# FFN down projection: three instead of two pairs per half as block products, their operands in two tiles each, and the turn of the PSUM sets advanced at each half's end

## The chip, the core and the metric

The kernel runs on one core of a Trainium2 chip. The metric is the time of one execution on the device, in microseconds (us); lower is better. TensorE (PE) multiplies matrices, VectorE (DVE) and ScalarE (ACT) work element by element, GpSimd (POOL) has little to do here, and SyncE (SP) issues the DMAs in the order in which they stand in its queue. Each engine takes its instructions in program order and waits on semaphores.

## The reference

Two decoder layers over 256 tokens of width 2048, in fp32. Layer 0 mixes tokens by sparse attention, layer 1 by an mLSTM; each is followed by a feed-forward part (FFN) of width 8192, and that part is what the change touches:

```python
hn = rms_norm(h, norm_ffn[i])
h = h + jnp.square(jax.nn.relu(hn @ ffn_w_up[i])) @ ffn_w_down[i]
```

## The kernel before

The program is written with a tile framework: tiles come from pools with a fixed number of buffers, a new tile of a tag waits until the oldest one of that tag is read for the last time, and a scheduler sets the order of the instructions on each engine at build time. So matmuls of different pairs may stand interleaved on PE, as long as their operands' order allows it.

Every fp32 product is made of three fp32r products: `split` makes a high part on ACT (a cast, L136) and a low part on DVE (a subtraction, L137), and PE multiplies high by high, high by low and low by high, each as a matmul of 128x512.

The FFN of a layer goes in four **quarters** of 2048 of its 8192 hidden columns. For each quarter, four calls of `project_t` make the up projection of 512 hidden columns each; their results leave PSUM as eight **pairs** of 256 hidden columns (`lhs`). Then the down projection of the quarter runs in two **halves** of 1024 output columns (`down_chunk`): a first half and a second half. In a half the eight pairs are added up in four PSUM banks `C` (2 token blocks x 2 column blocks of 512).

- A **plain pair** takes two loads of 512 KB (`w`, 5 buffers), each split into `wh` and `wl` (4 buffers each), and 24 matmuls (L494 to L496).
- A **block pair** (its number stands in `SEVEN`) takes one load of 1 MB (`sw`, one buffer) and a two-by-two block scheme with 7 products instead of 8: three subtractions on DVE make the sums of weight blocks (`st`, L478 to L480), `split` makes `sh` and `sl` of the 4 blocks in `sw` and of the 3 in `st`, and 21 matmuls follow. Three of its products go to `C` and four to a second set of banks, `S`, which all block pairs of a half share. After the half's last block pair, `S` is combined into a tile `e` and added to the residual `h` (`early`, L526 to L530 and L578). Tile `e` has the tag of `sw`, so it stands in the one buffer of `sw`.

The eight PSUM banks are two sets of four, `acc` and `acx`. `banks()` hands them out in turn by flipping `turn[0]`; a `project_t` takes one set, a half takes two (`C`, then `S`). At the end of a half, `C` is added to `h` (L274, in the last quarter L568 to the output).

The last quarter of layer 0's FFN goes without block pairs (`mix` is false), in four calls of `project`. So 7 quarters have halves, 14 in all. The loads for the first block pair of a quarter are issued during the up projection before it.

Of the kernel before, what the change touches and what calls it, by code (L numbers as in the profile page):

```python
# [10 lines left out]
F32R = mybir.dt.float32r  # L11
# [5 lines left out]
P = 128  # L17
# [14 lines left out]
TAKEN = -3.4e38  # L32
OUT = -1.0e30
RC, IC = 32, 16
SEVEN = (2, 5)


@with_exitstack
def trunk_kernel(ctx: ExitStack, tc, x, norm_mix, norm_ffn, att_w_in, att_q_gain, att_k_gain,
# [14 lines left out]
    n = [0]  # L54

    def uid(s):
        n[0] += 1
        return f"{s}_{n[0]}"
# [76 lines left out]
    def split(hi, lo, src):  # L135
        nc.scalar.copy(hi, src)  # L136
        nc.vector.tensor_tensor(lo, src, hi.bitcast(F32), op=ALU.subtract)  # L137
# [35 lines left out]
    turn = [0]  # L173
# [283 lines left out]
    def ffn(nm, up, down, nxt, pool, last=False):  # L457
# [14 lines left out]
        def seven(down, r0, n0):  # L472

            w = pool.tile([P, 4, 512], F32, tag="sw", name=uid("sw"))
            nc.sync.dma_start(w.rearrange("p (k n) f -> p k (n f)", k=2),
                              down[r0:r0 + 256, n0:n0 + 1024].rearrange("(k p) f -> p k f", p=P))
            t = pool.tile([P, 3, 512], F32, tag="st", name=uid("st"))
            nc.vector.tensor_tensor(t[:, 0:2], w[:, 1::2], w[:, 0:2], op=ALU.subtract)  # L478
            nc.vector.tensor_tensor(w[:, 1], w[:, 3], t[:, 0], op=ALU.subtract)
            nc.vector.tensor_tensor(t[:, 2], w[:, 2], w[:, 1], op=ALU.subtract)  # L480
            hi = pool.tile([P, 7, 512], F32R, tag="sh", name=uid("sh"))
            lo = pool.tile([P, 7, 512], F32R, tag="sl", name=uid("sl"))
            split(hi[:, :4], lo[:, :4], w)
            split(hi[:, 4:], lo[:, 4:], t)
            return hi, lo

        def down_chunk(lhs, q, n0, early, evac):

            C = banks()
            S = None  # L490
            first, final = min(SEVEN), max(SEVEN)

            def three(o, ah, al, hi, lo, start, stop):
                nc.tensor.matmul(o, ah, hi, start=start, stop=False, skip_group_check=True)  # L494
                nc.tensor.matmul(o, ah, lo, start=False, stop=False, skip_group_check=True)  # L495
                nc.tensor.matmul(o, al, hi, start=False, stop=stop, skip_group_check=True)  # L496

            for p in range(8):
                r0 = q * 2048 + 256 * p
                if p not in SEVEN:  # L500
                    a = lhs[p]
                    for k in range(2):
                        w = wp.tile([P, 2, 512], F32, tag="w", name=uid("w"), bufs=5)
                        nc.sync.dma_start(w, down[r0 + P * k:r0 + P * (k + 1), n0:n0 + 1024].rearrange(
                            "p (n f) -> p n f", n=2))
                        wh = wp.tile([P, 2, 512], F32R, tag="wh", name=uid("wh"), bufs=4)
                        wl = wp.tile([P, 2, 512], F32R, tag="wl", name=uid("wl"), bufs=4)
                        split(wh, wl, w)
                        for m in range(2):
                            ms = slice(m * P, (m + 1) * P)  # L510
                            for n in range(2):
                                three(C[2 * m + n], a[:, 0, k, ms], a[:, 1, k, ms], wh[:, n], wl[:, n],
                                      p == 0 and k == 0, p == 7 and k == 1)
                    continue
                if p == first:
                    S = banks()
                hi, lo = seven(down, r0, n0)
                vh, vl = lhs[p]

                for o, s, b, own in ((C[2], 2, 2, 0), (S[0], 0, 0, 1), (C[3], 6, 3, 0), (S[2], 4, 1, 1),  # L520
                                     (S[1], 3, 4, 1), (S[3], 5, 5, 1), (C[0], 1, 6, 0)):
                    three(o, vh[:, s], vl[:, s], hi[:, b], lo[:, b], bool(own and p == first), bool(own and p == final))
                if p == final:
                    e = pool.tile([P, 4, 512], F32, tag="sw", name=uid("e"))
                    u2 = t2k([P, 512], F32, "u2")
                    nc.scalar.copy(e[:, 2], S[0])  # L526
                    nc.vector.tensor_tensor(u2, S[2], e[:, 2], op=ALU.add)
                    nc.vector.tensor_tensor(e[:, 3], S[1], u2, op=ALU.add)
                    nc.vector.tensor_tensor(e[:, 0], S[3], u2, op=ALU.add)
                    nc.vector.tensor_tensor(e[:, 1], S[1], e[:, 0], op=ALU.add)  # L530
                    for m in range(2):
                        early(m, e[:, 2 * m:2 * m + 2])
            for m in range(2):
                for n in range(2):
                    evac(m, n, C[2 * m + n])

        for q in range(4):
            lhs, half = [], []
# [2 lines left out]
            def evac_up(b, p):  # L541
# [5 lines left out]
                if b % 2 == 0:  # L547
                    return
                if mix and len(lhs) in SEVEN:
                    y4 = pool.tile([P, 8, P], F32, tag="y4", name=uid("y4"))  # L550
# [207 lines left out]
    n0 = Norm(0)  # L758
# [53 lines left out]
```

## Time and profile before

| what | value |
|---|---|
| time, median of 3 runs | 2133.13 us (2132.56 to 2135.68) |
| the profiled execution's own time | 2133.99 us |
| its span in the profile | 2131.7 us |
| busy PE / DVE / ACT | 2114.1 us (99%) / 1424.9 us (67%) / 1045.3 us (49%) |
| mean granted clock of PE | 0.998 |

The span runs from the first to the last instruction; some 2.3 us lie around it. Matmuls are pipelined: a record of a 128x512 matmul lasts about 390 ns, while one follows the other after about 230 ns. So the busy time of PE hides what one matmul costs; it is read from a stretch with a known number of matmuls.

### The profile page before, as it was taken

The page shows a single profiled execution, that of the slowest core. Times are in us where ns is not written, and L with a number is a line of the kernel's source. Part 1 is how long each engine was busy: PE and PEld are TensorE (multiplying, and loading weights), DVE is VectorE, ACT ScalarE, POOL GpSimd, SP SyncE. Part 2 cuts the span into 40 slices and gives each one's busy share as a digit, 9 for nine tenths or more (in the row PEclk, how much of TensorE's full clock was granted, in tenths as well). Part 3 has the DMA queues.
Part 4 walks back from the last instruction along what each step waited for, and adds up shares of the span by engine and source line. Part 5 has one row for each costly group of instructions (what it writes and reads, how often), then busy time and mean ns, then how long its engine had stood idle before and what let it go on. Part 6 is the DMA issues. An engine that isn't in the chain of part 4 may idle for free.

```text
span 2131.7 us, 27757 instructions
## 1 busy us (share of the span) xinstructions
PE 2114.1 (99%) x10664; PEld 1797.7 (84%) x10664; DVE 1424.9 (67%) x1962; ACT 1045.3 (49%) x1350; POOL 14.0 (1%) x20
## 2 busy tenths in 40 slices
PE   9999999999999999999999999999999999999999
PEld 8988888888888888888999888888878888878887
DVE  5697676668668667655654565766677577668666
ACT  6556554544444454444554545545445444444543
POOL 0000000000000000000011000000000000000000
PEclk9999999999999999999999999999999999999999
DMA  7665366656655755665567655566567556656654
GB/s 233 188 180 151 118 213 188 191 171 213 190 168 186 219 173 176 188 188 186 169 183 210 171 167 169 192 201 190 160 196 215 179 183 207 188 162 217 190 164 142
DMA packets 178803, 393.06 MB, mean 184 GB/s; under 512 B 12336, under 2 KB 29168, under 8 KB 178672
## 3 DMA queue, kind: packets, MB, share of 16 engines
q1 hardware_dynamic: 178624, 391.29, 59.4%
q8 instruction: 83, 1.36, 0.3%
q14 instruction: 48, 0.39, 0.1%
q10 hardware_dynamic: 48, 0.02, 0.0%
HBM read 389.16 MB, written 2.10 MB: 184 GB/s over the span
## 4 chain that ended last, share of the span: by engine, by line
PE 94%; DMA 3%; DVE 2%; issue 1%; ACT 0%; SPq 0%; DVEq 0%
PE acc L195 13%; PE acx L195 12%; PE acc L168 10%; PE acc L167 10%; PE acc L169 10%; PE acc L494 7%; PE acc L495 7%; PE acc L496 7%; PE acx L197 6%; PE acc L197 6%; DMA sw<-in_ffn_w_down_dram 2%; PE acx L496 1%; PE acx L495 1%; PE acx L494 1%; DVE h L578 1%
## 5 line engine op out<-in xcount | busy, mean ns | idle before, releaser
L137 DVE TENSOR_TENSOR wl<-w,wh 128x1024 fp32r<-128x1024 f32 (+3 forms) x696 | 834.4, 1204 | 558.6 <-ACT wh L136 554.4
L136 ACT CAST wh<-w 128x1024 fp32r<-128x1024 f32 (+3 forms) x696 | 715.9, 1033 | 857.2 <-PE acc L496 229.3
L195 PE MATMUL acc<-xT,wh 128*128 128x512 f32 x1152 | 399.1, 396 | 4.4 <-DVE h L274 4.4
L195 PE MATMUL acx<-xT,wh 128*128 128x512 f32 x1152 | 402.3, 394 | 0.0
L197 PE MATMUL acx<-xT,wl 128*128 128x256 f32 x1152 | 321.0, 280 | 0.0
L197 PE MATMUL acc<-xT,wl 128*128 128x256 f32 x1152 | 312.4, 280 | 0.0
L495 PE MATMUL acc<-wl,hT 128*128 128x512 f32 x672 | 262.7, 391 | 0.0
L494 PE MATMUL acc<-wh,hT 128*128 128x512 f32 x672 | 259.9, 392 | 2.6 <-DVE h L274 2.2
L496 PE MATMUL acc<-wh,hT 128*128 128x512 f32 x672 | 262.1, 390 | 0.0
L195 PEld LDWEIGHTS acc<-xT,wh 128*128 128x128 f32 x1152 | 214.2, 188 | 55.0 <-issue 6.4
L195 PEld LDWEIGHTS acx<-xT,wh 128*128 128x128 f32 x1152 | 215.7, 187 | 49.6
L197 PEld LDWEIGHTS acx<-xT,wl 128*128 128x128 f32 x1152 | 217.1, 189 | 0.3
L197 PEld LDWEIGHTS acc<-xT,wl 128*128 128x128 f32 x1152 | 214.6, 189 | 3.0
L167 PE MATMUL acc<-wh,xT 128*128 128x512 f32 (+3 forms) x576 | 212.6, 372 | 2.1 <-ACT xT L230 2.1
L168 PE MATMUL acc<-wl,xT 128*128 128x512 f32 (+3 forms) x576 | 212.6, 371 | 0.0
L169 PE MATMUL acc<-wh,xT 128*128 128x512 f32 (+3 forms) x576 | 211.9, 371 | 0.0
L494 PEld LDWEIGHTS acc<-wh,hT 128*128 128x128 f32 x672 | 126.1, 188 | 34.4 <-issue 5.3
L495 PEld LDWEIGHTS acc<-wl,hT 128*128 128x128 f32 x672 | 126.2, 188 | 27.6 <-DVE wl L137 1.5
L496 PEld LDWEIGHTS acc<-wh,hT 128*128 128x128 f32 x672 | 126.2, 188 | 26.7
L167 PEld LDWEIGHTS acc<-wh,xT 128*128 128x128 f32 x576 | 108.1, 188 | 15.1 <-ACT xT L230 2.5
L169 PEld LDWEIGHTS acc<-wh,xT 128*128 128x128 f32 x576 | 108.3, 188 | 12.9 <-issue 0.3
L168 PEld LDWEIGHTS acc<-wl,xT 128*128 128x128 f32 x576 | 108.3, 188 | 12.8 <-issue 0.7
(242 smaller groups left out, 2237.6 us busy)
## 6 DMA issues: line engine op xcount, KB each, us to landing
w<-in_ffn_w_up_dram SPq DMA_DIRECT2D x256, 512.0 KB, 3.8
w<-in_ffn_w_down_dram SPq DMA_DIRECT2D x200, 512.0 KB, 3.9
w<-in_ml_w_in_dram SPq DMA_DIRECT2D x64, 512.0 KB, 3.8
sw<-in_ffn_w_down_dram SPq DMA_DIRECT2D x28, 1024.0 KB, 6.0
w<-in_att_w_in_dram SPq DMA_DIRECT2D x48, 512.0 KB, 4.4
w<-in_att_w_out_dram SPq DMA_DIRECT2D x32, 512.0 KB, 4.5
w<-in_ml_w_out_dram SPq DMA_DIRECT2D x32, 512.0 KB, 4.1
w<-in_ml_w_in_dram SPq DMA_DIRECT2D x32, 412.0 KB, 3.9
```

Of the source, the lines that this page charges most:

```text
L136: nc.scalar.copy(hi, src)
L137: nc.vector.tensor_tensor(lo, src, hi.bitcast(F32), op=ALU.subtract)
L167: nc.tensor.matmul(o, ah, wh[:, j, :width], start=(k == 0), stop=False)
L168: nc.tensor.matmul(o, ah, wl[:, j, :width], start=False, stop=False)
L169: nc.tensor.matmul(o, al, wh[:, j, :width], start=False, stop=(k == nk - 1))
L195: nc.tensor.matmul(acc[j], wh[:, kk % 2, js], a[:, :, k % 2], start=(k == 0), stop=False, skip_group_check=True)
L197: nc.tensor.matmul(acc[j][:, 1], wl[:, kk % 2, js], a[:, 0, k % 2], start=False, stop=(k == nk - 1), skip_group_check=True)
L494: nc.tensor.matmul(o, ah, hi, start=start, stop=False, skip_group_check=True)
L495: nc.tensor.matmul(o, ah, lo, start=False, stop=False, skip_group_check=True)
L496: nc.tensor.matmul(o, al, hi, start=False, stop=stop, skip_group_check=True)
L578: nc.vector.scalar_tensor_tensor(dst, e.rearrange("p n f -> p (n f)"), nm.r2[:, m:m + 1], dst, op0=ALU.mult, op1=ALU.add)
```

## The change

Pairs 1, 3 and 6 instead of 2 and 5 are block pairs. The operands of a block pair stand in two tiles each, `sh4`/`sl4` for the four weight blocks and `sh3`/`sl3` for the three sums, instead of one tile of seven. At the end of a half the turn is flipped once more, so that a half leaves with the other set next: a first half has `C` in `acc` and `S` in `acx`, a second half `C` in `acx` and `S` in `acc`. (Before, both halves had `C` in `acc`.) The low parts of the block pairs' left operands get a third buffer (`bufs=len(SEVEN)`).

```diff
--- before.py
+++ after.py
@@ -32,7 +32,7 @@
 TAKEN = -3.4e38
 OUT = -1.0e30
 RC, IC = 32, 16
-SEVEN = (2, 5)
+SEVEN = (1, 3, 6)
 
 
 @with_exitstack
@@ -478,11 +478,13 @@
             nc.vector.tensor_tensor(t[:, 0:2], w[:, 1::2], w[:, 0:2], op=ALU.subtract)
             nc.vector.tensor_tensor(w[:, 1], w[:, 3], t[:, 0], op=ALU.subtract)
             nc.vector.tensor_tensor(t[:, 2], w[:, 2], w[:, 1], op=ALU.subtract)
-            hi = pool.tile([P, 7, 512], F32R, tag="sh", name=uid("sh"))
-            lo = pool.tile([P, 7, 512], F32R, tag="sl", name=uid("sl"))
-            split(hi[:, :4], lo[:, :4], w)
-            split(hi[:, 4:], lo[:, 4:], t)
-            return hi, lo
+            parts = []
+            for n, src in ((4, w), (3, t)):
+                hi = pool.tile([P, n, 512], F32R, tag="sh%d" % n, name=uid("sh"))
+                lo = pool.tile([P, n, 512], F32R, tag="sl%d" % n, name=uid("sl"))
+                split(hi, lo, src)
+                parts += [(hi[:, b], lo[:, b]) for b in range(n)]
+            return parts
 
         def down_chunk(lhs, q, n0, early, evac):
 
@@ -514,12 +516,12 @@
                     continue
                 if p == first:
                     S = banks()
-                hi, lo = seven(down, r0, n0)
+                parts = seven(down, r0, n0)
                 vh, vl = lhs[p]
 
                 for o, s, b, own in ((C[2], 2, 2, 0), (S[0], 0, 0, 1), (C[3], 6, 3, 0), (S[2], 4, 1, 1),
                                      (S[1], 3, 4, 1), (S[3], 5, 5, 1), (C[0], 1, 6, 0)):
-                    three(o, vh[:, s], vl[:, s], hi[:, b], lo[:, b], bool(own and p == first), bool(own and p == final))
+                    three(o, vh[:, s], vl[:, s], *parts[b], bool(own and p == first), bool(own and p == final))
                 if p == final:
                     e = pool.tile([P, 4, 512], F32, tag="sw", name=uid("e"))
                     u2 = t2k([P, 512], F32, "u2")
@@ -533,6 +535,8 @@
             for m in range(2):
                 for n in range(2):
                     evac(m, n, C[2 * m + n])
+
+            turn[0] ^= 1
 
         for q in range(4):
             lhs, half = [], []
```

What the scheduler makes of it is shown at a second half (layer 0, first quarter); up to the rows shown the other six second halves have the same order.

DVE, before: rows from the last `wl` before the load of pair 2 is taken up. `st`, `sw`, `sl` are pair 2's, `wl` those of plain pairs, and `h<-acc` adds the first half's `C`.

```order
L137 TENSOR_TENSOR wl_4257<-w_4254,wh_4256 128x1024
L137 TENSOR_TENSOR wl_4275<-w_4272,wh_4274 128x1024
L478 TENSOR_TENSOR st_4332<-sw_4330 128x1024
L274 SCALAR_TENSOR_TENSOR h<-acc_3947,r_630_3130,h 128x512
L479 TENSOR_TENSOR sw_4330<-sw_4330,st_4332 128x512
L137 TENSOR_TENSOR wl_4293<-w_4290,wh_4292 128x1024
L274 SCALAR_TENSOR_TENSOR h<-acc_3948,r_630_3130,h 128x512
L274 SCALAR_TENSOR_TENSOR h<-acc_3949,r_630_3130,h 128x512
L480 TENSOR_TENSOR st_4332<-sw_4330 128x512
L274 SCALAR_TENSOR_TENSOR h<-acc_3950,r_630_3130,h 128x512
L137 TENSOR_TENSOR sl_4337<-sw_4330,sh_4336 128x2048
```

DVE, after: from the last `wl` before pair 1 of the second half. `st_4304`, `sw_4302`, `sl_4309`, `sl_4313` are pair 1's, `st_4375`, `sw_4373`, `sl_4380` pair 3's; `wl_4411` and `wl_4429` are pair 4's.

```order
L137 TENSOR_TENSOR wl_4358<-w_4355,wh_4357 128x1024
L478 TENSOR_TENSOR st_4304<-sw_4302 128x1024
L137 TENSOR_TENSOR wl_4411<-w_4408,wh_4410 128x1024
L479 TENSOR_TENSOR sw_4302<-sw_4302,st_4304 128x512
L480 TENSOR_TENSOR st_4304<-sw_4302 128x512
L137 TENSOR_TENSOR wl_4429<-w_4426,wh_4428 128x1024
L137 TENSOR_TENSOR sl_4309<-sw_4302,sh_4308 128x2048
L137 TENSOR_TENSOR sl_4313<-st_4304,sh_4312 128x1536
L478 TENSOR_TENSOR st_4375<-sw_4373 128x1024
L479 TENSOR_TENSOR sw_4373<-sw_4373,st_4375 128x512
L480 TENSOR_TENSOR st_4375<-sw_4373 128x512
L137 TENSOR_TENSOR sl_4380<-sw_4373,sh_4379 128x2048
```

The additions of `C` have moved ahead of the block pair, two `wl` stand within its subtractions, and pair 3's subtractions follow on pair 1's `sl` at once, where pair 5's came after four `wl`.

PE, before: the second half where the first products with pair 2's low part stand (`sl_4337`); `wh_4310` is pair 1's. Ahead of these rows stand 41 matmuls of the half.

```order
L494 MATMUL acc_4253<-wh_4310,hT_3334 128x512
L494 MATMUL acx_4327<-sh_4336,vh_3528 128x512
L494 MATMUL acx_4329<-sh_4336,vh_3528 128x512
L495 MATMUL acx_4326<-sl_4337,vh_3528 128x512
L496 MATMUL acx_4326<-sh_4336,vl_3529 128x512
L495 MATMUL acx_4328<-sl_4337,vh_3528 128x512
```

PE, after: pair 1 in the second half. Ahead of these rows stand 33 matmuls of the half, 24 of pair 0 and 9 of pairs 2 and 4; `wh_4428` and `wl_4429` are pair 4's, `sh_4308`/`sl_4309` and `sh_4312` pair 1's.

```order
L496 MATMUL acx_4259<-wh_4428,hT_3734 128x512
L497 MATMUL acx_4259<-wl_4429,hT_3734 128x512
L498 MATMUL acx_4259<-wh_4428,hT_3734 128x512
L496 MATMUL acx_4260<-sh_4308,vh_3338 128x512
L496 MATMUL acc_4298<-sh_4308,vh_3338 128x512
L496 MATMUL acx_4261<-sh_4308,vh_3338 128x512
L496 MATMUL acc_4300<-sh_4308,vh_3338 128x512
L496 MATMUL acc_4299<-sh_4312,vh_3338 128x512
L496 MATMUL acc_4301<-sh_4312,vh_3338 128x512
L496 MATMUL acx_4258<-sh_4312,vh_3338 128x512
L497 MATMUL acx_4260<-sl_4309,vh_3338 128x512
L498 MATMUL acx_4260<-sh_4308,vl_3339 128x512
```

PE, after: pair 3 of the same half. Ahead of these rows stand 75 matmuls of the half's 183, behind them 99; `sh_4379`, `sh_4383` and `sl_4380` are pair 3's, `wh_4446` is pair 5's.

```order
L496 MATMUL acx_4260<-sh_4379,vh_3543 128x512
L496 MATMUL acc_4298<-sh_4379,vh_3543 128x512
L496 MATMUL acx_4261<-sh_4379,vh_3543 128x512
L496 MATMUL acc_4300<-sh_4379,vh_3543 128x512
L496 MATMUL acx_4259<-wh_4446,hT_3744 128x512
L496 MATMUL acc_4299<-sh_4383,vh_3543 128x512
L496 MATMUL acc_4301<-sh_4383,vh_3543 128x512
L496 MATMUL acx_4258<-sh_4383,vh_3543 128x512
L497 MATMUL acx_4260<-sl_4380,vh_3543 128x512
```

Before, 42 matmuls of the half stood ahead of these first products of a block pair with its four blocks' sums, and 44 ahead of the first with a low part. Now 36 stand ahead of the first block product (24 of pair 0, 12 of pairs 2 and 4), 43 ahead of the first with a low part, and pair 3's first stands behind 75.

SP, before: the loads of the second half's pairs 2 and 5 (`sw`) among those of plain pairs (`w`).

```order
L504 DMA w_4363<-in_ffn_w_down_dram 128x1024
L475 DMA sw_4330<-in_ffn_w_down_dram 128x2x1024
L504 DMA w_4381<-in_ffn_w_down_dram 128x1024
L504 DMA w_4399<-in_ffn_w_down_dram 128x1024
L504 DMA w_4417<-in_ffn_w_down_dram 128x1024
L475 DMA sw_4435<-in_ffn_w_down_dram 128x2x1024
```

SP, after: the loads of the second half's pairs 1, 3 and 6.

```order
L506 DMA w_4444<-in_ffn_w_down_dram 128x1024
L475 DMA sw_4302<-in_ffn_w_down_dram 128x2x1024
L506 DMA w_4462<-in_ffn_w_down_dram 128x1024
L506 DMA w_4524<-in_ffn_w_down_dram 128x1024
L506 DMA w_4542<-in_ffn_w_down_dram 128x1024
L145 DMA w_4568<-in_ffn_w_up_dram 128x2x512
L475 DMA sw_4373<-in_ffn_w_down_dram 128x2x1024
L475 DMA sw_4480<-in_ffn_w_down_dram 128x2x1024
```

The load of pair 1 stands where that of pair 2 stood or a row later, and those of pairs 3 and 6 follow each other.

## Rows read from the trace of the kernel before

**Rows 1.** The page: its head, busy time of PE, first line of the chain

```profile
span 2131.7 us, 27757 instructions
...
PE 2114.1 (99%) x10664; PEld 1797.7 (84%) x10664; DVE 1424.9 (67%) x1962; ACT 1045.3 (49%) x1350; POOL 14.0 (1%) x20
...
PE 94%; DMA 3%; DVE 2%; issue 1%; ACT 0%; SPq 0%; DVEq 0%
```

**Rows 2.** Windows, PE alone, the fourteen halves: length, busy (x matmuls), granted clock, DMA

```profile
418.07:460.99 42.92, 42.68 (x188) 1.00 0.52 170
460.99:505.12 44.13, 43.11 (x186) 1.00 0.60 193
...
770.75:813.46 42.71, 42.70 (x188) 1.00 0.51 169
...
1907.09:1951.47 44.38, 43.09 (x187) 1.00 0.60 191
...
2083.62:2126.54 42.92, 42.92 (x186) 1.00 0.35 116
sum 607.26, PE 600.25; mean PE 42.87
```

**Rows 3.** Timeline, PE, end of a second half: start, length, what; idle before

```profile
503.71 0.39 PE L496 MATMUL acc<-wh,hT 128*128 128x512 f32 x1
505.12 0.47 PE L195 MATMUL acc<-xT,wh 128*128 128x512 f32 x1 [1.02 <-DVE h L274]
```

**Rows 4.** Timeline, DVE, around the boundary of the first quarter's halves

```profile
451.75 1.28 DVE L578 SCALAR_TENSOR_TENSOR h<-e,r,h 128x1024 f32<-128x1024 f32 x1
...
458.96 1.22 DVE L478 TENSOR_TENSOR st<-sw 128x1024 f32<-128x1024 f32 x1 [1.30 <-DMA sw<-in_ffn_w_down_dram]
...
460.76 0.68 DVE L479 TENSOR_TENSOR sw<-sw,st 128x512 f32<-128x512 f32 x1
...
465.08 2.28 DVE L137 TENSOR_TENSOR sl<-sw,sh 128x2048 fp32r<-128x2048 f32 x1
...
468.42 1.75 DVE L137 TENSOR_TENSOR sl<-st,sh 128x1536 fp32r<-128x1536 f32 x1
...
473.57 1.22 DVE L478 TENSOR_TENSOR st<-sw 128x1024 f32<-128x1024 f32 x1 [1.65 <-DMA sw<-in_ffn_w_down_dram]
474.71 2.35 DVE L137 TENSOR_TENSOR wl<-w,wh 128x1024 fp32r<-128x1024 f32 x2
476.98 0.69 DVE L479 TENSOR_TENSOR sw<-sw,st 128x512 f32<-128x512 f32 x1
```

**Rows 5.** Timeline, ACT, same stretch

```profile
461.48 1.91 ACT L136 CAST sh<-sw 128x2048 fp32r<-128x2048 f32 x1 [2.35 <-DVE sw L479]
...
477.83 1.92 ACT L136 CAST sh<-sw 128x2048 fp32r<-128x2048 f32 x1 [2.38 <-DVE sw L479]
479.65 1.47 ACT L136 CAST sh<-st 128x1536 fp32r<-128x1536 f32 x1
481.03 1.05 ACT L136 CAST wh<-w 128x1024 fp32r<-128x1024 f32 x1
```

**Rows 6.** Timeline, SP's DMA issues, same stretch

```profile
453.11 0.38 SPq L475 DMA_DIRECT2D sw<-in_ffn_w_down_dram  x1
...
467.39 0.38 SPq L475 DMA_DIRECT2D sw<-in_ffn_w_down_dram  x1
```

**Rows 7.** Tile sw, all its loads: issue to landing

```profile
DMA to landing us min/median/max: 5.6/6.0/6.9
```

**Rows 8.** Windows, all engines, one second half: PE, PEld, DVE, ACT, POOL

```profile
460.99:505.12 44.13, 43.11 (x186) 34.69 (x187) 34.45 (x33) 19.50 (x17) 0.00 (x0) 1.00 0.60 193
```

**Rows 9.** Timeline, PE, a wait in the attention part

```profile
235.69 1.22 PE L444 MATMUL aux<-pT,v 128*128 128x256 f32 x2 [2.00 <-ACT pT L442]
```

**Rows 10.** Windows, all engines, after that wait and after the wait of rows 3

```profile
235.47:238.88 3.41, 3.19 (x11) 2.69 (x12) 1.02 (x4) 0.87 (x3) 0.00 (x0) 0.50 0.71 218
...
505.10:508.50 3.40, 3.38 (x18) 2.76 (x19) 3.40 (x5) 2.85 (x2) 0.00 (x0) 1.00 0.22 39
```

## Prediction

> **What bounds the kernel now.** I read the page first: PE is busy 99% of the span of 2131.7 us and has 94% of the chain that ended last [rows 1]. A busy PE says little, since records overlap, so I cut the fourteen halves apart: a window from the first matmul of each half to the first behind it [rows 2]. The reader is to see that lengths differ while the number of matmuls does not: 42.71 us for the shortest, 44.38 for the longest, at a granted clock of 1.00 throughout. The shortest, 42.71 / 186 = 0.230 us a matmul, is PE at its pace. What the others have more stands at their ends: the first matmul behind a half waits for DVE's addition of `C` out of the same banks, 1.02 us in the case shown [rows 3]. Within the halves PE waits for nothing. So PE's count of matmuls and those ends are what the change can give back; what it can cost is a block pair whose operands come late. For that I read DVE, ACT and SP at the boundary between two halves [rows 4 to 6].
>
> **The profiled execution's own time** is 2134.0 us, 0.9 above the median of the runs. The sum is made against it.
>
> **Fewer matmuls.** One more block pair in 14 halves saves 14 x 3 = 42 matmuls (the order of PE has 42 rows fewer): 42 x 0.230 = 9.6 us. No added work is on PE. Bounds: the same, since PE waits nowhere inside a half. The Trainium skill (TensorE: Matmul & The Clock Gate, section Back-to-back issue gap) gives about 216 ns for a 512-column matmul; by it the saving would be 9.1 us. The trace has 230, and that is used.
>
> **The turn of the banks.** The second half's `C` is now the set that was `S`, emptied by `early` a plain pair earlier, and the next up projection takes the set that was `S` of the second half. In [rows 4] the last read for `early` is over at 451.75 + 1.28 = 453.03, two plain pairs ahead of the second half's first matmul at 460.99 [rows 2]; with one plain pair between, some 2.3 us ahead (worked out below). So the waits at the ends go: 607.26 less 7 x 42.71 and 7 x 42.92 (the shortest first half and the last second half, which has nothing behind it) is 7.9 us; less 14 x 42.71 it is 9.3. I take 8.6.
>
> **The added work on DVE and ACT** is hidden as work: a block pair for a plain one adds about 1.22 + 0.68 + 0.68 + 2.28 + 1.75 - 2 x 1.2 = 4.2 us of DVE [rows 4], and a second half has 34.5 of DVE in 44.1 [rows 8]; 38.7 of 42.0 still fits. It costs nothing unless it stands in a chain. It does:
>
> **The second half's chain.** `sw` has one buffer. Pair 1's load waits until `e`, in the same buffer, is read; pair 3's waits until pair 1's `sl` is made. Before, four plain pairs lay between the half's last block pair and the next half's first (5 to 2), now two (6 to 1); before, two lay between the block pairs of a half, now one between 1 and 3. Let H be the time of a second half's first matmul.
> - `e` was free 460.99 - 453.03 = 8.0 us ahead of it, of which 0.2 is that boundary's wait (42.92 against 42.71 in [rows 2]). A plain pair less is 24 x 0.230 = 5.5 us: now free at H - 2.3.
> - From there to L478: 453.03 to 458.96 is 5.9; from the end of an `sl` (465.08 + 2.28 = 467.36) to 473.57 it is 6.2 [rows 4, 6]; all loads land in 5.6 to 6.9, median 6.0 [rows 7]. I take 6.0: L478 of pair 1 at H + 3.7.
> - L478 and the `wl` behind it take 1.14 each back to back (473.57 to 476.98 for one and two `wl`), L479 0.68: over at H + 6.7. ACT's cast of 2048 takes 1.91 (H + 6.8 to 8.7) [rows 5], DVE's `sl` 2.28: over at H + 11.0. ACT is free for it: the `wh` ahead in its order waits for pair 0's second tile, 24 matmuls after H, and is over at about H + 6.7.
> - Pair 3's load then starts: L478 at H + 17.0, L479 over at H + 18.8, cast of 2048 to H + 20.8. In ACT's order one `wh` (1.05) stands ahead of the cast of 1536 (1.47): over at H + 23.2, PE can go on at H + 23.3.
> - PE has by its order 80 matmuls to put ahead of that product, 80 x 0.230 = 18.4 us. So it waits **4.9 us** in all: some 1.2 around pair 1 (the `wl` behind L480, then `sh` and `sl`), some 2.4 at pair 3's `sh` of four blocks, some 1.3 at that of three.
> - Behind it, 103 matmuls, 23.7 us. Pair 6's load waits for pair 3's `sl` (about H + 23.1), its `sl` comes about 12 us later at H + 35, and PE gets to its products with `sl` at about H + 38. No further wait.
>
> Seven second halves: 7 x 4.9 = 34.3 us. Bounds: both loads at 5.6 give 4.1 a half, both at 6.9 give 6.7, so 29 to 47. Queued behind the waiting loads on SP are the loads of pairs 5 and 7 and of the next up projection; the latter are needed some 20 us later.
>
> **First halves** get no such wait: their loads of pairs 1 and 3 and the sums are made during the up projection; only pair 3's cast waits, for pair 1's first 12 products, 36 matmuls or 8.3 us into the half, and `sl` is over 4.3 us later, at 12.6, while PE needs it after 75, at 17.2. Pair 6's load starts at 12.6 and its `sl` is made at about 25, needed after 138 matmuls, at 31.7. I take nothing; the cover is 4.6 us at pair 3 and 6.7 at pair 6.
>
> **The clock.** After a wait of 2.00 us in the attention part [rows 9] the granted clock is 0.50 in the next 3.41 us, and after the wait of 1.02 it is 1.00 [rows 10]. The waits of some 2.4 us lie near the first. A stretch of 3.41 us at 1.2 instead of 2.4 GHz costs at most 1.7 us; much of it would fall into the wait of 1.3 that follows. I take 0.5 a half, 3.5 us; bounds 0 and 11.9.
>
> **Sum:** 2134.0 - 9.6 - 8.6 + 34.3 + 3.5 = 2153.6, or 2153 against the median: slower by 0.9%.
>
> **Rivals.**
> - *The loads come sooner, and it is faster.* Saved are 18.2 us, so the change pays where a second half waits less than 2.6 us, that is where each of the two loads takes at most 4.8 us up to L478 instead of 6.0. For it: the SP queue has few other loads in flight there. Against it: 28 loads of 28 took 5.6 or more [rows 7]. With no wait at all: 2134.0 - 18.2 = 2115.8. The Trainium skill (DMA: Bandwidth & Descriptors, section Anatomy of one DMA) gives, for DMAs that GpSimd prepares, a fit of 2.0 us plus the bytes at 436 GB/s; by it 1 MB would take 4.4 us, the wait 1.7 and the kernel about 2128, an estimate that the measured loads speak against.
> - *The clock falls in full each time.* 2134.0 - 18.2 + 34.3 + 11.9 = 2162. For it: [rows 9, 10]. Against it: PE has work between the two waits. The Trainium skill (TensorE: Matmul & The Clock Gate, section HAM oscillation) warns that waits between bursts of matmuls bring the half clock back each time; the trace agrees for the one wait shown, with 0.50.
> - *First halves wait too*, because DVE's queue is late with pair 3: at 2 us in each of seven, 2168. Against it: the cover of 4.6 us.
> - *The turn gives nothing*, another wait taking its place at the ends: 2162. Against it: `early` is over 2.3 us ahead.
>
> **How the numbers follow.** Forecast 0.68; sooner loads 0.13 (of which 0.09 ends faster, 0.04 near none); clock in full 0.11; first halves 0.05; turn 0.03. Within 0.2% (4.3 us) is about what a measurement here can't tell from no change: faster 0.09, same 0.05, slower 0.86. The likeliest alone has 2146 to 2162. The range 2140 to 2167 takes in the bounds of the loads, the clock and the turn, and leaves out about 0.1 below and 0.06 above.
>
> **What would show it.** Fourteen windows as in [rows 2]: first halves at about 42.0 us with 183 matmuls, second halves at 47 or more; PE's waits for ACT's `sh`, some 2.4 and 1.3 us, seven times each, at pair 3; no wait for L274 at the ends; SP waiting at `sw` for the update of `h` and for `sl`; granted clock of 0.50 in some second halves. Second halves below 44.5 would make me wrong, and first halves above 43 would add a cause.

## The result and the profile after

The changed kernel takes **2165.0 us** (median of 4 runs, 2162.7 to 2165.8) against 2133.8 (2132.6 to 2135.7) before: a ratio of 1.0144, 95% interval 1.0129 to 1.0159. The forecast was 2153, with a range of 2140 to 2167. The profiled execution took 2164.5 us, with a span of 2162.7.

The first part of the page answers to [rows 1]: PE is busy 98% of a longer span, and DVE has 67 us more to do.

```profile
span 2162.7 us, 27699 instructions
PE 2124.0 (98%) x10622; PEld 1800.2 (83%) x10622; DVE 1491.8 (69%) x2032; ACT 1062.5 (49%) x1350; POOL 14.0 (1%) x20
```

The fourteen halves, cut as in [rows 2], show where the time is. The columns are the window, its length, PE's busy time in it with the matmuls on record, the granted clock, and the DMA engines' share and GB/s.

```profile
418.37:460.37 42.00, 42.00 (x186) 1.00 0.48 155
460.37:510.48 50.11, 45.67 (x185) 0.93 0.51 166
...
1748.60:1797.47 48.87, 44.66 (x185) 0.97 0.50 168
...
2067.05:2109.03 41.98, 41.98 (x185) 1.00 0.47 156
2109.03:2157.05 48.02, 44.54 (x184) 0.96 0.38 117
sum 639.47, PE 612.13; mean PE 43.72
```

Each first half takes 42.0 us, without a wait. Each second half takes 48.0 to 50.1. Length less busy time is idle time: 50.11 - 45.67 = 4.4 us in the first of them. Busy time above 42.0 is work at a slower pace, or short gaps that the matmuls' long records cover: 45.67 - 42.0 = 3.7 us. Over the seven second halves (345.5 us, 318.2 of it busy) that makes 27.3 us idle and 24.2 us of slower work and covered gaps. PE's waits say for what, in us in all, times, and longest:

```profile
PE acx L496 <- ACT sh L136: 19.4, 7, 3.2
PE acx L497 <- DVE wl L137: 7.1, 7, 1.4
```

And SP's queue waits at the loads of `sw` (L475) for the low parts of the block pair ahead, and for the update of `h` by `e`, as the chain has it:

```profile
SPq L475 <- DVE sl L137: 111.7, 28, 6.4
SPq L475 <- DVE h L582: 62.5, 12, 5.4
```

The line for L274 behind the halves, 1.02 us in [rows 3], is gone. Around the wait for `sh` in the first quarter, 3.0 us, the granted clock falls to half, 1.2 GHz, and returns:

```profile
475.00:481.79 6.79, 4.67 (x21) 1.00 0.26 93
481.79:488.62 6.83, 5.90 (x14) 0.50 0.34 95
488.62:495.45 6.83, 6.83 (x31) 1.00 0.62 215
```

Such a stretch stands in all seven second halves, 6.83 us long in five (the halves at 0.93) and 3.41 in two (0.96 and 0.97). DVE's timeline at that boundary answers to [rows 4]; H, the second half's first matmul, is at 460.37:

```profile
456.97 1.28 DVE L582 SCALAR_TENSOR_TENSOR h<-e,r,h 128x1024 f32<-128x1024 f32 x1
...
464.75 1.23 DVE L478 TENSOR_TENSOR st<-sw 128x1024 f32<-128x1024 f32 x1 [1.23 <-DMA sw<-in_ffn_w_down_dram]
...
469.68 2.29 DVE L137 TENSOR_TENSOR sl<-sw,sh 128x2048 fp32r<-128x2048 f32 x1
...
478.65 1.23 DVE L478 TENSOR_TENSOR st<-sw 128x1024 f32<-128x1024 f32 x1 [5.01 <-DMA sw<-in_ffn_w_down_dram]
479.91 0.69 DVE L479 TENSOR_TENSOR sw<-sw,st 128x512 f32<-128x512 f32 x1
```

and ACT's cast of pair 3's four blocks behind it, to [rows 5], over at 482.67, is what PE waited for:

```profile
480.77 1.90 ACT L136 CAST sh<-sw 128x2048 fp32r<-128x2048 f32 x1 [9.73 <-DVE sw L479]
```

The chain stands as forecast and runs a little late: e read at H - 2.1 (forecast H - 2.3), pair 1's L478 at H + 4.4 (3.7), its low parts over at H + 11.6 (11.0), pair 3's L478 at H + 18.3 (17.0; 17.2 to 18.3 in the seven second halves), its cast over and PE going on at H + 22.3 (20.8).

### The profile page after: what moved, and what is told of

Its sections match the earlier page's. It is cut to its first block, busy times and chain, and to the rows that moved or that the text cites. A ratio compares the mean times of both kernels' runs of the same rounds, so it can differ in the third digit from the quotient of the medians.

```text
span 2162.7 us, 27699 instructions
## 1 busy us (share of the span) xinstructions
PE 2124.0 (98%) x10622; PEld 1800.2 (83%) x10622; DVE 1491.8 (69%) x2032; ACT 1062.5 (49%) x1350; POOL 14.0 (1%) x20
## 4 chain that ended last, share of the span: by engine, by line
PE 89%; DMA 4%; DVE 4%; ACT 2%; issue 1%; DVEq 0%; SPq 0%; ACTq 0%
PE acc L195 12%; PE acx L195 12%; PE acc L167 10%; PE acc L168 10%; PE acc L169 9%; PE acc L197 6%; PE acx L197 6%; DMA sw<-in_ffn_w_down_dram 4%; PE acc L496 4%; PE acc L498 4%; PE acc L497 4%; PE acx L496 3%; PE acx L497 3%; PE acx L498 3%; ACT sh L136 1%; DVE h L582 1%
## 5 line engine op out<-in xcount | busy, mean ns | idle before, releaser
L137 DVE TENSOR_TENSOR wl<-w,wh 128x1024 fp32r<-128x1024 f32 (+3 forms) x668 | 800.3, 1204 | 483.5 <-ACT wh L136 479.4
L136 ACT CAST wh<-w 128x1024 fp32r<-128x1024 f32 (+3 forms) x668 | 687.3, 1032 | 784.1 <-PE acc L169 221.6
L195 PE MATMUL acc<-xT,wh 128*128 128x512 f32 x1152 | 403.8, 396 | 0.0
L197 PE MATMUL acc<-xT,wl 128*128 128x256 f32 x1152 | 320.9, 280 | 0.0
L195 PEld LDWEIGHTS acc<-xT,wh 128*128 128x128 f32 x1152 | 215.9, 188 | 50.1
L136 ACT CAST sh<-sw 128x2048 fp32r<-128x2048 f32 x42 | 80.1, 1907 | 167.6 <-DVE sw L479 155.5
L137 DVE TENSOR_TENSOR sl<-sw,sh 128x2048 fp32r<-128x2048 f32 x42 | 96.3, 2292 | 47.3 <-ACT sh L136 46.5
L497 PE MATMUL acx<-wl,hT 128*128 128x512 f32 x280 | 110.2, 394 | 7.1 <-DVE wl L137 7.1
L496 PE MATMUL acx<-wh,hT 128*128 128x512 f32 x280 | 111.0, 396 | 0.0
L498 PE MATMUL acx<-wh,hT 128*128 128x512 f32 x280 | 109.4, 391 | 0.0
L497 PE MATMUL acc<-wl,hT 128*128 128x512 f32 x280 | 109.4, 391 | 0.0
```

The costliest lines, as they stand in the source:

```text
L195: nc.tensor.matmul(acc[j], wh[:, kk % 2, js], a[:, :, k % 2], start=(k == 0), stop=False, skip_group_check=True)
L197: nc.tensor.matmul(acc[j][:, 1], wl[:, kk % 2, js], a[:, 0, k % 2], start=False, stop=(k == nk - 1), skip_group_check=True)
```

## The experiments

In the table "second half" is the mean length of the seven, "idle" the mean of length less PE's busy time, both from one profile each. For no turn the profiled execution took 2160.7 us, 5.5 below the median, for e in the high parts' buffer 2142.4, 5.9 above it. All runs differ from the changed kernel by the edits named alone, and by what the scheduler makes of them: the order on the engines changes with an edit. The kernel before took 2131.6 to 2134.2 us (medians) beside them.

| run | time, us (range) | second half | idle |
|---|---|---|---|
| changed kernel | 2165.0 (2162.7 to 2165.8) | 49.4 | 3.9 |
| pairs 2 and 5 | 2124.2 (2123.4 to 2125.6) | 42.5 | 0 |
| no turn | 2166.2 (2160.7 to 2170.8) | 48.1 | 4.3 |
| one tile | 2168.7 (2166.2 to 2169.4) | 49.7 | 4.4 |
| wait filled | 2147.7 (2146.2 to 2149.0) | 47.6 | 1.5 |
| e in the high parts' buffer | 2136.6 (2134.4 to 2142.5) | 45.3 | 2.0 |
| e in the low parts' buffer | 2119.6 (2117.5 to 2122.9) | 42.7 | 0.3 |
| pairs 1, 3, 5 | 2158.6 (2156.7 to 2158.8) | 48.8 | 4.3 |
| pairs 1, 3, 5, e in the low parts' | 2131.4 (2125.6 to 2136.0) | 43.0 | 0.4 |
| loads of sw by GpSimd | 2159.4 (2158.4 to 2162.6) | 48.4 | 4.2 |
| loads of sw split | 2162.4 (2159.8 to 2168.9) | 48.8 | 4.1 |
| split, e in the low parts' | 2131.2 (2128.1 to 2136.1) | 43.9 | 1.2 |
| two buffers for sw | 2157.7 (2157.4 to 2160.1) | 42.1 | 0 |

### The parts of the change

```diff
-SEVEN = (1, 3, 6)
+SEVEN = (2, 5)
```

> Pairs 2 and 5 as before, with two tiles of operands and the turn. Turn theory: the waits at the half ends, 8.6 us in all, go and nothing else changes: 2125 us (2123 to 2127), fourteen halves of 42.7 us. Rival: the waits at the ends were hiding something that is late next (the load behind e, or the low parts of pair 2), and the time stays within 2 us of before, 2132 to 2136.

Measured: 2124.2 us, a ratio of 0.9953 (0.9941 to 0.9965). All fourteen halves take 42.5 us, with no idle time at their ends:

```profile
417.59:460.11 42.52, 42.52 (x188) 1.00 0.51 169
460.11:502.58 42.47, 42.47 (x187) 1.00 0.62 197
```

So the turn (with the two tiles) is worth 9.4 us where nothing else is late, and in the halves nothing takes the place of the waits. There it gives 12.4 us (607.3 to 594.9); the five up projections that follow a second half within a layer take 3.0 us more together (449.0 to 452.0).

```diff
-            turn[0] ^= 1
```

> Three block pairs and two tiles, without the turn at the end of a half. Full theory: the waits at the half ends come back with their whole price of 8.6 us: 2173.6. Offset theory: only the seven ends behind second halves cost their 0.6 us each, since in front of a second half the wait moves H while the chain of loads counts from the end of e, so it is taken off the wait behind it: 2165 + 4 = 2169 us. Rival: the turn is worth nothing here, 2165.

Measured: 2166.2 us. The interval of its ratio (1.0130 to 1.0167, that is 2161 to 2169 us) leaves out 2173.6, and holds both the rival's 2165 and the offset theory's 2169. The waits for L274 are back, behind six second halves and not in front of any, but 2 us each:

```profile
PE acc L195 <- DVE h L274: 12.0, 6, 2.5
...
456.75:504.04 47.29, 43.55 (x184) 1.00 0.52 178
819.29:868.24 48.95, 44.77 (x185) 0.97 0.49 168
```

That the time hardly moves doesn't make the turn worth nothing, as the rival has it: without the turn no wait inside a half is above 1.4 us, where the changed kernel has 3.3, and the granted clock is 1.00 in five of seven second halves, where the changed kernel has none. In and just behind the second halves it is at half for four stretches of 3.41 us, two of them behind the wait at a half's end, against 41 us in the changed kernel. The mean clock is 0.996 in this execution, and 0.993 and 0.992 in those of 2167.8 and 2170.8 us. The order of PE's instructions differs between the two kernels as well, so how much of the 12 us the clock alone gives back stays open.

```diff
-            parts = []
-            for n, src in ((4, w), (3, t)):
-                hi = pool.tile([P, n, 512], F32R, tag="sh%d" % n, name=uid("sh"))
...
+            hi = pool.tile([P, 7, 512], F32R, tag="sh", name=uid("sh"))
+            lo = pool.tile([P, 7, 512], F32R, tag="sl", name=uid("sl"))
+            split(hi[:, :4], lo[:, :4], w)
+            split(hi[:, 4:], lo[:, 4:], t)
+            parts = [(hi[:, b], lo[:, b]) for b in range(7)]
```

> Pairs 1, 3, 6 and the turn, but one tile of seven blocks for the high parts and one for the low parts. Tile theory: the cast of pair 3's four blocks must wait until all products of pair 1 are through, and the first product of pair 3 waits for both casts instead of one; the wait at pair 3 grows by the second cast (some 1.5 to 2.4 us) in each second half: 2165 + 7 x 2 = 2179 us, first halves still 42.0 us if their cover of 4.6 us holds. Rival: the second cast is made while PE's clock is at half and its products would have waited for the low parts anyway, so the split is worth nothing: 2163 to 2167.

Measured: 2168.7 us, 3.7 above the changed kernel, with intervals that overlap (1.0145 to 1.0171 against 1.0129 to 1.0159). The split is worth some 4 us here, if anything; the expected 14 was wrong.

### The clock

`zr` is a tile of zeros:

```diff
+    zr = cp.tile([P, P], F32R, name="zr")
+    nc.vector.memset(zr.bitcast(F32), 0.0)
...
                 parts = seven(down, r0, n0)
                 vh, vl = lhs[p]
+                if p == 3 and n0:
+                    for _ in range(12):
+                        nc.tensor.matmul(C[3], zr, wl[:, 1], start=False, stop=False, skip_group_check=True)
```

> Twelve matmuls that add products with a tile of zeros to a bank of C (nothing in the result changes) stand in each second half behind pair 2, 12 x 0.228 = 2.7 us of work ahead of pair 3's wait of 3.2 us. Clock theory: the drop of the granted clock to 0.50 at that wait is caused by the wait; with 0.5 us of it left the clock stays at 1.00, and though the program has 84 matmuls more a second half is shorter by some 3.3 us: 46.1 us, the kernel 2142 us. Rival: the drop comes from elsewhere (the block pair's products, the load of the engines), and the filled wait changes nothing: 2165 us. Rival: the dummies come on top, since pair 3's chain moves with them: 2165 + 19 = 2184 us.

Measured: 2147.7 us, 17.4 less than the changed kernel, with 84 matmuls (19.1 us) more on PE. The granted clock is 1.00 in all seven second halves, of which the first is:

```profile
461.77:509.49 47.72, 46.19 (x197) 1.00 0.52 173
```

So the drop of the clock is caused by the wait. The expected 2142 was 6 too low: a second half takes 47.6 us instead of 46.1, since besides 1.5 us of idle time some 1.4 us of short gaps remain at full clock (46.1 busy less 12 x 0.228 for the dummies is 43.4, not 42.0). The matmuls' long records cover these gaps. The second halves have 12.0 of the 17.4 us; in the profiled executions, 15.5 us apart, the other 3.4 lie outside the halves.

How the waits and the clock share the changed kernel's loss is read from its own matmuls, from one start to the next. At half clock they start 0.43 us apart, and not 0.23:

```profile
487.76 0.63 PE L498 MATMUL acc<-sh,vl 128*128 128x512 f32 x1
488.19 0.60 PE L497 MATMUL acx<-sl,vh 128*128 128x512 f32 x1
488.62 0.40 PE L498 MATMUL acx<-sh,vl 128*128 128x512 f32 x1
```

In the seven second halves 81 matmuls do so, which costs 16.2 us with those at the ends of the stretches. Gaps of 1 us and more from start to start, less 0.23 each, make 29.8 us, and short gaps around them 5.5. Together that is 51.5 us, what the seven are longer than 7 x 42.0: 35.3 us of waits, short gaps included, and 16.2 of the clock.

### The chain of loads

```diff
-                    e = pool.tile([P, 4, 512], F32, tag="sw", name=uid("e"))
+                    e = pool.tile([P, 4, 512], F32, tag="sh4", name=uid("e"))
```

> Chain theory: the second half waits because pair 1's load can't start before e, in the one buffer of sw, is read. With e in the buffer of the four-block high parts the load of pair 1 starts when pair 6's low parts of the first half are made, some 16 us before H, and pair 3's operands (load, three sums, cast) are there at about H + 13, while PE needs them at H + 18. All fourteen halves then take 42.0 us at a granted clock of 1.00, and the time is 2165.0 - 7 x 7.4 = 2113 us (2110 to 2118). Rival, queue theory: DVE or ACT is late by its own queue of work and the load only appears last; then second halves stay above 46 us and the time above 2140. Rival, clock theory: the half clock belongs to the block products and not to the wait; then the waits of some 4.1 us a half go and the clock's 3 us stay, 2136 us.

Measured: 2136.6 us. The chain theory has the larger part, 28 of 52 us, but not the whole. Pair 1's load was there 11 us ahead of H (461.74), and its low parts still came late, at H + 7.5. ACT's cast, which comes behind the last read of e, was over at H + 3.1; then four additions of `C` and a `wl` stood ahead of the low parts on DVE:

```profile
462.95 1.90 ACT L136 CAST sh<-sw 128x2048 fp32r<-128x2048 f32 x1
463.14 2.72 DVE L274 SCALAR_TENSOR_TENSOR h<-acc,r,h 128x512 f32<-128x512 f32 x4
...
466.91 2.29 DVE L137 TENSOR_TENSOR sl<-sw,sh 128x2048 fp32r<-128x2048 f32 x1
...
476.25 1.23 DVE L478 TENSOR_TENSOR st<-sw 128x1024 f32<-128x1024 f32 x1 [4.78 <-DMA sw<-in_ffn_w_down_dram]
```

Pair 3's load so began only then. The time is the clock theory's 2136, but not for its reason: four of the seven second halves have the same block products at 1.00, and what they have above 42.0 is waits. The same run warns about the clock: two halves with nearly equal waits (1.40 and 1.06 us, 1.31 and 1.07 between successive matmuls) have 1.00 and 0.96.

```profile
461.74:506.44 44.70, 42.59 (x184) 1.00 0.57 189
1554.39:1600.55 46.16, 44.14 (x184) 0.96 0.55 182
```

The next run differs from this one by `tag="sl4"` instead of `tag="sh4"`.

> As the run with e in the buffer of the four-block high parts, but e in that of the four-block low parts. There pair 1's load landed 11 us ahead of H, but its cast waited for e and its low parts stood on DVE behind the four additions of C to h, over only at H + 7.5, so pair 3 was late again. Queue theory: here the cast is made before e is read, and the low parts still stand behind those additions in DVE's order, over at about H + 6.4: 1.1 us sooner, so that of the 2.7 us of waits a second half some 1.1 go: 2128 us (2124 to 2132). Rival: the cast was what held them; low parts at H + 3 and no wait: 2113 us. Rival: no change, 2136.

Measured: **2119.6 us**, a ratio to the kernel before of 0.993 (0.9918 to 0.9942), the fastest of all here, and below the 2124 that the queue theory had as its lower bound. Six of seven second halves take 42.0 to 42.6 us. On DVE, H is at 461.84:

```profile
462.70 2.72 DVE L274 SCALAR_TENSOR_TENSOR h<-acc,r,h 128x512 f32<-128x512 f32 x4
465.34 2.28 DVE L137 TENSOR_TENSOR sl<-sw,sh 128x2048 fp32r<-128x2048 f32 x1
...
473.31 1.23 DVE L478 TENSOR_TENSOR st<-sw 128x1024 f32<-128x1024 f32 x1 [2.29 <-DMA sw<-in_ffn_w_down_dram]
```

The low parts stand behind the additions as expected, and are over at 467.62, H + 5.8. Pair 3's load then takes 5.7 us up to L478; in the run before it took 7.0 (469.20 to 476.25). 1.7 us sooner and 1.3 us faster is more than the 2.7 us of waits. (In the first six second halves that load takes 5.7 to 6.4 us here and 6.8 to 7.2 in the run before; why wasn't settled.) Only the last second half still has such waits, 46.11 us at 0.96. There that load takes 7.6 us (low parts over at 2073.85, L478 at 2081.46), and on SP four stores of the output stand right ahead of it, which no other half has; that they slow it was seen beside it only, not tried.

```profile
2069.70 2.77 SPq L574 DMA_DIRECT2D out_dram<-o  x4
2073.87 0.39 SPq L475 DMA_DIRECT2D sw<-in_ffn_w_down_dram  x1
```

```diff
-SEVEN = (1, 3, 6)
+SEVEN = (1, 3, 5)
```

> Pairs 1, 3 and 5 instead of 1, 3 and 6, all else as changed; e keeps its place in sw. Spacing theory: what was wrong is the two plain pairs left between pair 6 and the next half's pair 1. With 5 last, e is read one plain pair sooner, at about H - 7.6, so pair 1's load lands at H - 1.2, its low parts are made by H + 6, pair 3's load lands at H + 12.5 and its cast is over at H + 16.5, ahead of PE's need at H + 18.4. Fourteen halves of 42.0 us, clock 1.00: 2165.0 - 51.5 = 2113 us (2110 to 2120). Rival, cover theory: pairs 3 and 5 now stand as close as 1 and 3, a block pair's chain (load 6.4, sums 1.9, cast 1.9, low parts 2.3) is 12.5 us against 10.2 us of PE's 45 matmuls, and the wait only moves to pair 5, in first halves too: some 1 to 2 us in each of 14, 2125 to 2140. Rival: the spacing is of no account, and DVE's or ACT's load is: 2160 or more.

Measured: 2158.6 us. The spacing alone buys next to nothing, though pair 1's load lands as early as H + 1.1 (H is 461.93). What is late next is DVE's queue at the boundary:

```profile
463.00 1.23 DVE L478 TENSOR_TENSOR st<-sw 128x1024 f32<-128x1024 f32 x1 [0.37 <-DMA sw<-in_ffn_w_down_dram]
464.14 1.41 DVE L274 SCALAR_TENSOR_TENSOR h<-acc,r,h 128x512 f32<-128x512 f32 x2
465.46 1.22 DVE L137 TENSOR_TENSOR wl<-w,wh 128x1024 fp32r<-128x1024 f32 x1
466.60 0.69 DVE L479 TENSOR_TENSOR sw<-sw,st 128x512 f32<-128x512 f32 x1
467.20 1.22 DVE L137 TENSOR_TENSOR wl<-w,wh 128x1024 fp32r<-128x1024 f32 x1
468.33 0.69 DVE L480 TENSOR_TENSOR st<-sw 128x512 f32<-128x512 f32 x1
469.27 2.29 DVE L137 TENSOR_TENSOR sl<-sw,sh 128x2048 fp32r<-128x2048 f32 x1 [0.25 <-ACT sh L136]
```

Three subtractions of 2.6 us take from 463.00 to 469.02 here, since two additions of `C` and two `wl` stand between them. The low parts are over at H + 9.6 instead of H + 6, and in all seven second halves a wait of 0.6 to 1.1 us for the cast of pair 5's three blocks comes on top, in two of them one of 1.5 and 1.7 us for its four. That is the cover theory's wait, though first halves, at 42.0 us, have none.

Pairs 1, 3, 5 and `tag="sl4"` for e, together:

> Pairs 1, 3, 5 and e in the buffer of the four-block low parts. Queue theory: with 1, 3, 5 alone pair 1's load landed at H + 1.05, but its sums and low parts stood on DVE between the additions of C and the low parts of plain pairs, over only at H + 9.6; here the load is early, the sums stand ahead of H, and the low parts ahead of three of the four additions of C, over at about H + 3. Pair 3's operands are then there at H + 13.5 (needed at H + 18), pair 5's at H + 26 (needed at H + 28): fourteen halves of 42.0 us and 2113 to 2117 us. Rival, cover theory: pairs 3 and 5 stand too close for one buffer, and pair 5 waits some 1 to 2 us in second halves, with the clock at half behind it in some: 2122 to 2135.

Measured: 2131.4 us. Second halves are down to 43.0, which alone would give 2165.0 - 7 x 6.4 = 2120; in four of the seven pair 5 waits 0.5 to 0.9 us, with the clock at 1.00. The 11 us more lie in the up projections that follow a second half: the early low parts of the next quarter's pair 1 now stand on DVE ahead of a `wl` of the up projection, and PE waits there, in five places:

```profile
PE acc L197 <- DVE wl L137: 7.4, 5, 1.6
```

Those five stretches take 92.0 to 92.3 us each, the first of them 92.14, where the changed kernel has 89.1 in four and 90.4 in one: 13.6 us more, of which the 7.4 are the part that shows as idle time.

```profile
501.88:594.02 92.14, 90.62 (x513) 1.00 0.67 206
```

### The load itself

Loads of `sw` by `nc.gpsimd.dma_start` instead of `nc.sync.dma_start`:

> The loads of sw are issued by GpSimd instead of SP, with all else as changed. SP theory: behind the waiting load of sw the loads of w stand still on SP, and they then come in a bunch beside it and make it slow; on a queue of its own sw lands within 6.0 us or less, the w loads are early, the wait around pair 1 (1.2 to 1.6 us a second half) goes and that at pair 3 shrinks by 0.5 to 1: 2150 us. Chain theory: the load still starts only when its buffer is free, and lands no sooner; w loads that go on meanwhile take bandwidth from it: 2160 to 2172 us.

Measured: 2159.4 us, between the two theories and nearer to the chain's. Most of the wait for `sh` is gone, and waits for `wl` have come in its place (22.0 us in 16), so the idle time is as long. The load takes longer, 6.2 us in the median against 5.8:

```profile
sw<-in_ffn_w_down_dram POOLq DMA_DIRECT2D x42, 1024.0 KB, 6.2
```

```diff
-            nc.sync.dma_start(w.rearrange("p (k n) f -> p k (n f)", k=2),
-                              down[r0:r0 + 256, n0:n0 + 1024].rearrange("(k p) f -> p k f", p=P))
+            for k, queue in enumerate((nc.sync, nc.gpsimd)):
+                queue.dma_start(w[:, 2 * k:2 * k + 2], down[r0 + P * k:r0 + P * (k + 1), n0:n0 + 1024].rearrange(
+                    "p (n f) -> p n f", n=2))
```

> As changed, but each load of sw as two of 512 KB, one issued by SP, one by GpSimd. Queue theory: a load of 512 KB lands 4.0 us after its issue in the median, one of 1 MB in 5.8, so two at once land in some 4.0 to 4.5; two loads of the chain are 2 us shorter each, the waits of 4.3 us a second half fall below 1, and the clock stays at 1.00: 2118 us (2114 to 2125). Rival, shared engines: the same 16 DMA engines move the same bytes, the load lands in 5.8 to 6.6 as before, and the time is that of the changed kernel or some 5 us less, as with the loads on GpSimd alone (2159): 2157 to 2166.

Measured: 2162.4 us, no change beyond the uncertainty. The two halves land after 4.4 and 5.5 us:

```profile
sw<-in_ffn_w_down_dram SPq DMA_DIRECT2D x42, 512.0 KB, 4.4
sw<-in_ffn_w_down_dram POOLq DMA_DIRECT2D x42, 512.0 KB, 5.5
```

The later one decides, and it is 0.3 us sooner than one load of 1 MB. In the chain nothing is left of that: from the end of pair 1's low parts to pair 3's L478 the seven second halves take 5.5 to 7.3 us, where the changed kernel has 5.8 to 6.8. The Trainium skill (DMA: Bandwidth & Descriptors, section Issuing engines are not separate DMA queues) says that DMAs of all issuing engines run on the same 16 DMA engines and interleave there; the two landings agree.

Split loads and e in the low parts' buffer:

> Pairs 1, 3, 6, e in the buffer of the four-block low parts, and the load of sw in two halves on SP and GpSimd. That version without the split load took 2119.6 us, of which 4.1 us are the last second half's wait at pair 3 (1.3 and 1.1 us) and the half clock behind it. Queue theory: the load is 1.5 to 2 us shorter and the last half takes 42.0 us too: 2115 us. Shared engines: no change, 2119 to 2121.

Measured: 2131.2 us, 11.6 slower than with whole loads. Waits of up to 1.04 and 1.06 us at pair 3 are back in six of the seven second halves. In those six GpSimd's half of pair 3's load lands 6.5 to 7.6 us after its issue; in the seventh, without a wait (42.01 us), after 5.3. The whole load took 5.7 to 6.3, and 7.6 in the last second half. The two parts in the first second half:

```profile
sw<-in_ffn_w_down_dram SPq DMA_DIRECT2D x1, 512.0 KB, 4.2
sw<-in_ffn_w_down_dram POOLq DMA_DIRECT2D x1, 512.0 KB, 7.5
```

Why GpSimd's part is so late there wasn't settled.

### Two buffers

```diff
-            w = pool.tile([P, 4, 512], F32, tag="sw", name=uid("sw"))
+            w = pool.tile([P, 4, 512], F32, tag="sw", name=uid("sw"), bufs=2)
...
-                    e = pool.tile([P, 4, 512], F32, tag="sw", name=uid("e"))
+                    e = pool.tile([P, 4, 512], F32, tag="sl4", name=uid("e"))
...
-                        w = wp.tile([P, 2, 512], F32, tag="w", name=uid("w"), bufs=5)
+                        w = wp.tile([P, 2, 512], F32, tag="w", name=uid("w"), bufs=4)
...
-                    y4 = pool.tile([P, 8, P], F32, tag="y4", name=uid("y4"))
+                    y4 = pool.tile([P, 3, 512], F32, tag="st", name=uid("y4")).rearrange("p a f -> p (a f)")[:, :1024].rearrange("p (s t) -> p s t", s=8)
```

> Pairs 1, 3, 6 with the turn, e in the buffer of the four-block low parts, and two buffers for sw (room is made by four buffers instead of five for w, and by putting y4, which is used in the up projection only, in the buffer of st). Buffer theory: pair 3's load no longer waits for pair 1's low parts and pair 6's not for pair 3's, so that no load stands in a chain; fourteen halves of 42.0 us, the last second half too (46.1 with one buffer): 2115 us (2112 to 2118). Rival, shared engines and queues: the loads of sw now come earlier and collide with those of w, which have a buffer less, and DVE's queue is as full as before; waits for wl or for the up projection's wl come in their place, 2120 to 2135.

(The loads of the up projection have four buffers for `w` as well.)

Measured: 2157.7 us. Both theories missed the place. All seven second halves take 42.0 to 42.1 us, the last one too, and the first halves 47.4 to 48.5:

```profile
416.13:463.54 47.41, 44.28 (x186) 0.96 0.53 178
463.54:505.60 42.06, 42.06 (x184) 1.00 0.60 201
```

DVE shows why. The room came from putting `y4` into the buffer of `st`. The last read of `y4` (`vl`) is over 6.3 us into the first half, and only then can pair 1's sums begin, whose load had landed at 274.68:

```profile
421.36 1.08 DVE L137 TENSOR_TENSOR vl<-y,vh 128x896 fp32r<-128x896 f32 x1
...
422.96 1.22 DVE L478 TENSOR_TENSOR st<-sw 128x1024 f32<-128x1024 f32 x1
```

The run shows the mechanism from both sides. With the second buffer pair 3's load is issued 14.3 us ahead of H in all seven second halves, and the last one falls from 46.1 to 42.0 us; in the other six e's place had taken the waits away already. And a shared buffer makes such waits in first halves, at nearly the same price, 3.1 us idle and the clock.

## Why the prediction was right, and where it was off

- **Direction and mechanism: right.** The one buffer of `sw`, with e in it, holds back pair 1's load, and the chain then holds back pair 3. Taking e out removes the waits in six of seven second halves (2119.6 us), and the second buffer in the seventh too; the number of block pairs, DVE's added work and the split into two tiles, all there in those six, don't make them.
- **Fewer matmuls and the turn: right in sum, off in the parts.** The halves without their waits are 14 x 42.0 = 588.0 us against 607.3: 19.3 less, where 9.6 + 8.6 = 18.2 were forecast. With pairs 2 and 5 and the turn they take 594.9, so the turn (with the two tiles) gave 12.4 of it and the third block pair 6.9. The shortest half before, 42.71, taken for PE at its pace, still held some 0.2 us of gaps (42.5 with the turn); the two errors nearly cancel.
- **First halves: right.** No wait, 42.0 us.
- **Waits in second halves: right in size, partly by luck.** With the short gaps they cost 35.3 us; forecast 34.3, bounds 29 to 47. Of the three places in a half two showed in all seven, 0.8 to 1.6 us at the `wl` behind L480 and 2.3 to 3.3 at pair 3's `sh` of four blocks (from one matmul's start to the next, less 0.23): 28.7 us where 7 x 3.6 = 25.2 were forecast. The third, 1.3 at the `sh` of three blocks and 9.1 in all, stands in one of the seven alone, with 1.06: at half clock PE comes to it later. The 5.5 us of short gaps, which the forecast put at nothing, made up for most of that. The loads took 6.5 and 6.7 us up to L478 in the first quarter, 6.1 and 6.4 in the mean of the seven, where 6.0 was taken.
- **The clock: the term that was mis-sized.** I took 0.5 us a half, since a wait of 2.00 had cost one stretch of 3.41 us [rows 9, 10] and part of it would be hidden; 7 x 1.7 = 11.9 was the bound. It is 16.2 us, above the bound, though part of it was hidden as said: the third wait is gone in six halves. Five of the seven stretches were 6.83 us long, and PE was busy in 5.90 of the 6.83 shown. So the rival of the clock that falls in full, at 0.11 and 2162, is what came, and the likeliest case was 11 us too low mainly for that reason. The Trainium skill (TensorE: Matmul & The Clock Gate, section HAM oscillation) warns of just this, half clock again behind waits between bursts; the seven stretches at 0.50 and the filled wait at 1.00 agree. Not every wait brought it: behind 0.8 to 1.4 us and another 1.06, four halves of the run with e in the high parts' buffer stayed at 1.00.
- Sum of the measured terms: 2134.0 - 19.3 + 35.3 + 16.2 = 2166.2, and 1.7 less outside the halves (the other windows 1524.4 to 1523.2, the time around the span 2.3 to 1.8): 2164.5.
- **The range: held by 2 us.** 2165.0 lies inside 2140 to 2167, but above the 2146 to 2162 of the likeliest case alone; with the clock 4 us above its bound, it held because the other terms came near their middle.
- **Break-even: right for the loss as a whole.** I put it at 2.6 us of wait a second half. With 19.3 us saved it is 2.8, the clock's part included: with e in the high parts' buffer second halves are 3.3 us above 42.0 (in an execution 6 us above the median), and the kernel is 3 us slower than before; with e in the low parts' buffer they are 0.7 above, and it is 15 faster.

## What to carry to other kernels

Before a step is put closer to its like, count the chain through their shared buffer (last read, load, sums, cast, low parts) against the work that lies between, and look at every other tile that shares the tag: here one word, which buffer e stands in, decides between 31 us lost and 15 won. Count DVE's queue into that chain: a load that lands at a boundary waits behind whatever the boundary puts there. And price a wait of PE of 2 to 3 us with the half clock behind it, which here added nearly half to the waits' own cost (16.2 on 35.3).

## What the runs showed of the hardware that wasn't expected

- The kernel was faster with more work on PE: 84 matmuls of zeros in the waits took 17.4 us off.
- Nearly the same waits (1.4 and 1.06 us) left the granted clock at 1.00 in one half and brought it to 0.50 for a stretch in another of the same execution.
- A load of 1 MB for pair 3 of a second half took 5.7 us from issue to its first reader in one quarter and 7.6 in another of the same execution, and one split over two queues was hardly sooner (5.5 against 5.8 in the median), or later (7.5 for GpSimd's part beside 4.2 for SP's).
